# Two blocks on one core: the second block's two attentions as sequences of small tasks, and a margin on modelled times in the order of the first half's parts

## The chip, the cores and the metric

The kernel runs on one core of a Trainium2 chip. The metric is the time of one execution on the device in microseconds (us), lower is better. Each time below is from the chip: either a timed run, or one execution taken with the hardware profiler. The engines are named as in the profile: PE is TensorE's matrix multiply, PEld its weight load, DVE is VectorE, ACT ScalarE, POOL GpSimd, SP the engine whose queue issues nearly all DMAs.

## What is computed

1024 tokens of width 1024 go through two transformer blocks in float32. Block 1 mixes a recurrent branch with an attention branch and ends in a mixture of 32 experts; the change does not touch it. Block 2, cut to what matters:

```python
xn = rmsnorm(x, attn_norm_g)
qa, ka, va, qb, kb, vb, f_logit = split(xn @ w_in)          # 8 heads of 64 each; ka, va: 2 heads
out_a = swa_sinks_attention(rms(qa), rms(ka), va, sinks)    # window of 128 keys, a sink logit per head
out_b = forgetting_attention(rms(qb), rms(kb), vb, log_f)   # causal, logit += c[t] - c[s], c = cumsum(log_f)
x = x + concat(out_a, out_b) @ w_out
x = x + square(relu(rmsnorm(x) @ w_up)) @ w_down            # d_ff 4096
```

## The kernel before

**Matmuls.** Each float32 operand of a matmul is split into a rounded high half and a rounded remainder, and a product is three matmuls: high x high, high x low, low x high (`mm3`), accumulated in a bank of PSUM. The split is one copy on ScalarE and then one subtraction on VectorE (`split`, `split_T`), so each operand that TensorE reads has passed ScalarE and VectorE first, in that order. Weights stream from HBM by way of SP's queue in pieces of 512 KB and are split in the same way (128x1024 rows of the trace).

**The order.** The program's order on each engine is made when it is built. The kernel is written as tasks (Python generators with a priority, lower goes first). A task yields either a time or a condition. `Tasks.run` takes again and again the first task, by priority, whose condition holds and whose time is not after "now", the planner's clock of TensorE. That clock comes from a cost model with a fixed price for each instruction; `model.written(ap)` is the modelled time at which an operand is ready, `model.released(ap)` the time at which it may be overwritten. So `yield W(t.f())` before a matmul means: put it into the order only when TensorE's clock has come to the operand's modelled time. Until then parts of other tasks are put there; the main task (dense matmuls, priority 9) nearly always has one. `Later` holds back instructions of the other engines, and DMAs, in the same way until the model says that they are ready. On the chip each engine works through its own queue in that order, and waits where an operand is later than was modelled.

**Block 2.** The tokens go in two halves of 512. The main task (`block2`) runs the projections of half 0 (`kvf`, `kb`, `qb`, `vb`, `qa`), then those of half 1, and stores the results in DRAM (`d_kva`, `d_kb`, `d_qb`, `d_qa` and others). Beside it run tasks:

- `fox(0)`, priority 1, the forgetting attention of half 0. It starts when `qb` and `vb` are done. Per pair of heads (4 pairs) and pair of query blocks (2) it makes scores (matmuls of 64 rows), adds a bias row that is loaded from `d_cb` and masked by GpSimd, takes the exponential, and hands two pieces (one for each head) to `fox_values`. That task, priority 1, scales a piece by the reciprocal of its sum (VectorE), waits, transposes its probabilities in chunks of 256 keys (TensorE, into banks 4 and 5), splits them, multiplies them with V, and stores the output to `d_mix`. 16 pieces in a half. Four probability buffers (`p`) go round between the two tasks.
- `swa(0)`, priority 2, the windowed attention of half 0. It starts when `qa` is done, and is one task: for each of the four blocks of 128 queries the scores of both groups of heads, then `values` of group 0, `values` of group 1, then the next block's scores. `values` scales, waits, transposes one or two chunks, waits, multiplies, waits, and stores the output to `d_mix`: 8 stores in a half. Two probability buffers (`nsr = 2`).
- `forget(1)`, priority 1: the cumulated log of the forget gates of half 1, written to `d_cb`.
- `mixin(0)`, priority 4, added when `vb` of half 1 is done. It allocates 8192 words in one piece (`TT`), loads the eight tiles of `d_mix` one after the other and splits them. With it done, `out2(0)` may run in the main task: the output projection, which stands after the first two of the four `qa` tiles of half 1. Its matmuls stand in TensorE's queue in order, and nothing else of the main task can go ahead of it.

Then the last two `qa` tiles follow, and the MLP of half 0 (`mlp`), with `swa(1)`, after it `fox(1)`, and `mixin(1)` beside it. `fox(1)` needs the flag `swa1`. Then come `out2(1)` and the MLP of half 1, with no attention beside it.

On-chip memory is handed out by arenas: `F` (19872 words a partition, plain float32), `R` (16896 words, rounded) and two swing arenas `Z` (8192 words each) that `R` falls back on. A task starts only when `fits` says that its buffers can be had. While both attentions of half 0 run, `swa(0)` holds 6144 words of one swing arena, and the other one holds half 1's input.

The windowed attention's main loop before:

```python
        yield from prep(n0)
        for n in range(n0, n0 + 5):
            if n > n0 and nsr == 2:
                for kh in range(2):
                    yield from values(n - 1, kh)
            if n < n0 + 4:
                yield from scores(n)
                if n + 1 < n0 + 4:
                    yield from prep(n + 1)
```

Of the kernel before, what the change touches and what calls it, by code (L numbers as in the profile page):

```python
# [657 lines left out]
class Kern:  # L658
# [1348 lines left out]
    def block2(self):  # L2007
# [60 lines left out]
        for half in range(2):  # L2068
# [95 lines left out]

    def swa(self, half):
# [10 lines left out]
        S, tb, ob = Banks(self.psum, 2, 2), Banks(self.psum, 4, 2), self.bank(6)  # L2176
# [5 lines left out]
        st, orr = Ring(F, 4, 32), Ring(F, 1, 512)  # L2182
        self.sp.dma_start(kv.f(nk, 256), self.KVA[k0 * 128:(n0 + 4) * 128].rearrange("(a p) c -> p a c", p=128))
        qs, Q, P = {}, {}, {}
# [21 lines left out]
        sr = Ring(F, nsr, 1024)  # L2206
# [12 lines left out]
        def scores(n):  # L2219
# [5 lines left out]
            bs, ss = [sr.next(), sr.next()], [st.next(), st.next()]  # L2225
# [19 lines left out]
            for kh in range(2):  # L2245
                P[n, kh] = (bs[kh], ss[kh], w)

        def values(n, kh):
            b, s, w = P.pop((n, kh))
# [19 lines left out]
            for c in range(nb):  # L2269
                vv = V.r(nk, 2, 128)[:, n + 1 - nb + c - k0, kh]  # L2270
                self.mm(ob, vv, ts[c].r(2, 512)[:, 0], c == 0, False)
                self.mm(ob, vv, ts[c].r(2, 512)[:, 1], False, c == nb - 1)
            yield W(ob)
            t = orr.next()
# [5 lines left out]
        yield from prep(n0)  # L2280
        for n in range(n0, n0 + 5):
            if n > n0 and nsr == 2:
                for kh in range(2):
                    yield from values(n - 1, kh)
            if n < n0 + 4:
                yield from scores(n)
                if n + 1 < n0 + 4:
                    yield from prep(n + 1)
            if n > n0 and nsr == 4:
                for kh in range(2):  # L2290
                    yield from values(n - 1, kh)
        for b in (kT, V, qr, qT, sr, pt, st, orr) + ((bias, snk, g) if half else ()):
# [3 lines left out]
    def fox(self, half):  # L2296

        F, R, v, act, gp = self.F, self.R, self.v, self.act, self.gp
        W, free = self.model.written, self.model.released
# [14 lines left out]
        steps = [(pr, gi, hh) for pr, gi in units for hh in range(2)]  # L2314
        self.tasks.add(self.fox_values(half, steps, fx), 1)
# [59 lines left out]
        for n, (pr, gi) in enumerate(units):  # L2375
# [32 lines left out]
            for hh in range(2):  # L2408
                fx["ready"][2 * n + hh] = (ss[hh], out[hh])
# [5 lines left out]
    def fox_values(self, half, steps, fx):  # L2415
        F, R, v, act, gp = self.F, self.R, self.v, self.act, self.gp
        W, free = self.model.written, self.model.released
        NKB = 4 * (half + 1)
# [410 lines left out]
```

## Time and profile before

| | us |
|---|---|
| median of 3 timed runs (lowest, highest) | 2784.4 (2781.36, 2788.27) |
| the profiled execution, its own time | 2780.47 |
| span of that execution, first to last instruction | 2778.7 |
| mean granted clock of TensorE over the span | 0.979 |

The profile is of one execution. A busy time of an engine is the sum of its instructions' durations; PE's are pipelined, so that a PE that is always busy shows 100%. The granted clock is the share of TensorE's full clock that the chip let through in a stretch: 1.00 is 2.4 GHz, 0.50 is 1.2 GHz, and a value between them is a stretch that had both. Times in the timelines count from the start of the span. L234 and L270 are lines of the helper that records every instruction, so nearly all rows carry one of these two lines and are told apart by operands and shapes. Operands are named by their arena: `rounded` is R, `swing` Z, `exact` F, `psum` PSUM; names that begin with `d_` are tensors in DRAM.

In the trace, matmuls `psum<-rounded,swing 128x512` are the projections and `out2`, `psum<-rounded 64x..` are scores of the forgetting attention, `psum<-rounded 128x128` and `128x256` its multiplications with V, `psum<-swing 64x..` scores of the first half's windowed attention, `psum<-swing 128x512` its multiplications with V, and `psum<-exact 128x128` transposes.

### The profile page before, as it was taken

How to read it: one execution, taken by the hardware profiler on the slowest of the kernel's cores; microseconds unless marked ns; L12 is line 12 of the kernel's file. 1: busy time of each engine (PE TensorE's matmuls, PEld its weight loads, DVE VectorE, ACT ScalarE, POOL GpSimd, SP SyncE). 2: the span in 40 equal slices, each digit the busy share in tenths (PEclk: the TensorE clock that was granted, in tenths of full speed). 3: DMA queues.
4: the chain of work that ended last, by engine and by line, in shares of the span. 5: the costliest groups of instructions: out<-in, count | busy, mean ns of one | idle time of the engine just before them, and what ended most of it. 6: DMA issues, size and time to landing. Idle time of an engine off the chain costs nothing. (4 is left out here: it accounts for less than half of the span.)

```text
span 2778.7 us, 37066 instructions
## 1 busy us (share of the span) xinstructions
PE 2642.0 (95%) x13090; PEld 2146.4 (77%) x13090; DVE 1785.0 (64%) x3100; ACT 1507.8 (54%) x2455; POOL 422.5 (15%) x486
## 2 busy tenths in 40 slices
PE   8899999999999799999997898889999999999999
PEld 6677777778888678888886776667887778888887
DVE  4574443652575699999986647755666666546683
ACT  4144444543443588888886646645545555345542
POOL 0540002430121113111111322200000000000000
PEclk9999999999999899999999999899999999999999
DMA  5333223435556899999997444444234443443330
GB/s 180 119 98 92 92 74 106 133 107 174 192 178 226 281 344 376 373 361 358 365 358 261 165 143 138 128 146 150 88 113 145 132 144 120 148 140 122 122 120 32
DMA packets 272030, 496.22 MB, mean 179 GB/s; under 512 B 30337, under 2 KB 127265, under 8 KB 271841
## 3 DMA queue, kind: packets, MB, share of 16 engines
q1 hardware_dynamic: 261184, 471.78, 49.7%
q0 software_dynamic: 9216, 16.81, 2.4%
q10 hardware_dynamic: 1440, 5.24, 0.5%
q8 instruction: 103, 1.69, 0.3%
q14 instruction: 87, 0.70, 0.1%
HBM read 440.05 MB, written 70.45 MB: 184 GB/s over the span
## 5 line engine op out<-in xcount | busy, mean ns | idle before, releaser
L234 PE MATMUL psum<-rounded,swing 128*128 128x512 f32 (+1 forms) x3552 | 868.4, 396 | 23.4 <-ACT swing L270 10.3
L234 PE MATMUL psum<-rounded 128*128 128x512 f32 (+6 forms) x3672 | 791.8, 386 | 24.3 <-DVE rounded L270 11.3
L234 PE MATMUL psum<-swing,rounded 128*128 128x512 f32 (+1 forms) x3328 | 785.0, 389 | 0.4 <-DVE swing L270 0.4
L234 PEld LDWEIGHTS psum<-rounded,swing 128*128 128x128 f32 x3552 | 651.5, 192 | 166.3 <-issue 18.4
L234 PEld LDWEIGHTS psum<-rounded 128*128 128x128 f32 (+1 forms) x3672 | 609.4, 189 | 174.0 <-issue 19.8
L270 DVE TENSOR_TENSOR rounded<-exact,rounded 128x1024 fp32r<-128x1024 f32 (+1 forms) x483 | 572.2, 1206 | 234.4 <-ACT rounded L270 226.8
L234 PEld LDWEIGHTS psum<-swing,rounded 128*128 128x128 f32 x3328 | 603.8, 189 | 129.2 <-issue 6.5
L270 ACT ACTIVATE rounded<-exact 128x1024 fp32r<-128x1024 f32 (+1 forms) x483 | 500.6, 1045 | 296.6 <-PE psum L234 221.1
L234 PE MATMUL psum<-exact 128*128 128x128 f32 (+6 forms) x2198 | 312.9, 284 | 78.0 <-DVE exact L270 23.4
L234 PEld LDWEIGHTS psum<-exact 128*128 128x128 f32 (+2 forms) x2198 | 262.5, 163 | 141.4 <-DVE exact L270 36.1
L270 POOL TENSOR_TENSOR exact<-exact 128x1 f32<-128x1 f32 (+6 forms) x272 | 261.2, 964 | 721.4 <-DMA exact<-d_cb 416.6
L270 ACT ACTIVATE exact<-psum 128x512 f32<-128x512 f32 (+4 forms) x290 | 160.1, 553 | 366.0 <-PE psum L234 297.3
L270 ACT ACTIVATE exact<-exact 128x512 f32<-128x512 f32 (+11 forms) x398 | 247.1, 632 | 175.7 <-DVE exact L270 147.4
L270 DVE TENSOR_TENSOR rounded<-swing,rounded 128x1024 fp32r<-128x1024 f32 x217 | 256.4, 1218 | 37.9 <-ACT rounded L270 37.0
L270 ACT ACTIVATE rounded<-swing 128x1024 fp32r<-128x1024 f32 x217 | 223.8, 1065 | 36.3 <-PE psum L234 26.4
L270 DVE TENSOR_TENSOR exact<-psum,exact 128x512 f32<-128x512 f32 x156 | 107.3, 688 | 143.3 <-PE psum L234 111.8
L270 DVE TENSOR_TENSOR exact<-exact 128x512 f32<-128x512 f32 (+9 forms) x250 | 154.6, 628 | 42.4 <-POOL exact L270 24.1
L270 DVE CUSTOM_DVE_ANT_0 exact<-psum,exact 128x512 f32<-128x512 f32 (+5 forms) x224 | 127.8, 593 | 80.4 <-PE psum L234 51.6
L270 POOL TENSOR_SCALAR exact<-exact 128x1 f32<-128x1 f32 (+4 forms) x134 | 42.6, 318 | 785.4 <-DVE exact L270 553.1
L270 DVE TENSOR_TENSOR swing<-psum,swing 128x512 fp32r<-128x512 f32 (+2 forms) x151 | 88.9, 615 | 95.1 <-ACT swing L270 94.7
L270 ACT ACTIVATE rounded<-psum 128x512 fp32r<-128x512 f32 (+2 forms) x190 | 88.1, 496 | 105.8 <-PE psum L234 105.2
L270 DVE TENSOR_TENSOR rounded<-psum,rounded 128x512 fp32r<-128x512 f32 (+2 forms) x190 | 101.7, 558 | 56.4 <-ACT rounded L270 56.3
(49 smaller groups left out, 1074.1 us busy)
## 6 DMA issues: line engine op xcount, KB each, us to landing
exact<-in_w_dram SPq DMA_DIRECT2D x188, 512.0 KB
swing<-in_w_dram SPq DMA_DIRECT2D x186, 512.0 KB
exact<-in_w_in_dram SPq DMA_DIRECT2D x72, 512.0 KB
exact<-in_w_down_dram SPq DMA_DIRECT2D x66, 512.0 KB
exact<-in_w_up_dram SPq DMA_DIRECT2D x62, 512.0 KB
exact<-in_w_out_dram SPq DMA_DIRECT2D x32, 512.0 KB
exact<-in_x_dram SPq DMA_DIRECT2D x16, 512.0 KB
d_g<-exact SPq DMA_DIRECT2D x32, 256.0 KB
```

The lines of the kernel that those rows point to most:

```text
L234: r = fn(*args, **kw)
L270: r = fn(*args, **kw)
```

## The change

It makes five edits, all of them in the order of the work:

1. `safe(half)`: in half 0, `W` is the operand's modelled time plus 600 ns, in the scores of both attentions and in both `values` tasks. In half 1 it stays as it was.
2. `swa` becomes three tasks: scores (priority 2), `swa_scale` (1) and `swa_values` (1), with four probability buffers instead of two.
3. `fox_values` gives its scaling to a task of its own, `fox_scale` (1). Neither scaling task has the margin.
4. In both `values` tasks a chunk's multiplication comes after the next chunk's transposes, and an output's evacuation (`finish`) after the transposes that follow its last multiplication; where the next piece is not scaled yet, both are done at once.
5. `mixin(0)` is added right after `qa` of half 0, and waits for `swa0` alone.

The diff, cut to its core:

```diff
--- before.py
+++ after.py
@@ -2085,7 +2085,6 @@
             if half == 0:
                 self.tasks.add(self.fox(0), 1)
             else:
-                self.tasks.add(self.mixin(0), 4)
                 nq = 2
...
             self.flag(f"qa{half}")
             if half == 0:
                 self.tasks.add(self.swa(0), 2)
+                self.tasks.add(self.mixin(0), 4)
...
+    def safe(self, half):
+
+        return self.model.written if half else lambda ap: self.model.written(ap) + 600.0
+
     def swa(self, half):
...
-        W, free = self.model.written, self.model.released
+        W, free = self.safe(half), self.model.released
...
-        nsr = 2
+        nsr = 4
...
-        yield lambda: (self.has(f"qa{half}") and self.ws.settled() and self.F.fits(256 * nk, 512, 512, 32, 32, 32, 32, 512, *[1024] * nsr) and
+        yield lambda: (self.has(f"qa{half}") and self.ws.settled() and self.F.fits(256 * nk, 512, 512, 32, 32, 32, 32, 512, *[1024] * (nsr - nk // 4)) and
...
-        sr = Ring(F, nsr, 1024)
+        sr = Slots(F, nsr, 1024)
+        sx = {"V": V, "k0": k0, "nk": nk, "sr": sr, "st": st, "pt": pt, "orr": orr, "ready": {}, "scaled": {}}
+        steps = [(n, kh) for n in range(n0, n0 + 4) for kh in range(2)]
+        self.tasks.add(self.swa_scale(steps, sx), 1)
+        self.tasks.add(self.swa_values(half, steps, sx), 1)
...
             for kh in range(2):
-                P[n, kh] = (bs[kh], ss[kh], w)
-
-        def values(n, kh):
-            b, s, w = P.pop((n, kh))
+                sx["ready"][n, kh] = bs[kh], ss[kh], w
+
+        yield from prep(n0)
+        for n in range(n0, n0 + 4):
+            yield from scores(n)
+            if n + 1 < n0 + 4:
+                yield from prep(n + 1)
...
+    def swa_scale(self, steps, sx):
+
+        v, act, snk, W = self.v, self.act, self.snk, self.model.written
+        for n, kh in steps:
+            yield lambda: (n, kh) in sx["ready"]
+            b, s, w = sx["ready"].pop((n, kh))
             f = s.f()
             x = b.f(4, 256)[:, :, :w]
             yield W(f)
...
             v.tensor_tensor(x, x, f[:, 12:16, None].to_broadcast([128, 4, w]), OP.mult)
-            yield W(b.f())
-            nb = w // 128
-            ts = []
-            for c in range(nb):
-                p, t = tb.next(), pt.next()
-                yield free(p)
-                for j in range(4):
-                    self.pe.transpose(p[:, j * 128:j * 128 + 128], b.f(4, 256)[:, j, c * 128:c * 128 + 128], self.ident)
-                self.split_T(p, t.r(2, 512)[:, 0], t.r(2, 512)[:, 1], t.f(2, 512)[:, 0])
-                ts.append(t)
-            yield max(W(ts[-1].f()), free(ob))
...
+            sx["st"].give(s)
+            sx["scaled"][n, kh] = b
+
+    def swa_values(self, half, steps, sx):
...
+        for n, kh in steps:
+            nb = 2 if n else 1
+            for c in range(nb):
+                if (n, kh) not in sx["scaled"]:
+                    yield from finish()
+                    yield from multiply()
+                    yield lambda: (n, kh) in sx["scaled"]
+                b = sx["scaled"][n, kh]
+                p, t = tb.next(), pt.next()
+                yield max(free(p), W(b.f()))
+                for j in range(4):
+                    self.pe.transpose(p[:, j * 128:j * 128 + 128], b.f(4, 256)[:, j, c * 128:c * 128 + 128], self.ident)
+                self.split_T(p, t.r(2, 512)[:, 0], t.r(2, 512)[:, 1], t.f(2, 512)[:, 0])
+                if c == nb - 1:
+                    sx["sr"].give(b)
+                yield from finish()
+                yield from multiply()
+                state[0] = (n, kh), c, nb, t
+        yield from finish()
+        yield from multiply()
+        yield from finish()
...
     def fox(self, half):
...
-        W, free = self.model.written, self.model.released
+        W, free = self.safe(half), self.model.released
...
+        fx["scaled"] = {}
+        self.tasks.add(self.fox_scale(steps, fx), 1)
         self.tasks.add(self.fox_values(half, steps, fx), 1)
...
+    def fox_scale(self, steps, fx):
+
+        v, W = self.v, self.model.written
         for n, (pr, gi, hh) in enumerate(steps):
             yield lambda: n in fx["ready"]
...
             v.reciprocal(f[:, 4:6], f[:, 2:4])
             for ii in range(2):
                 x = bs[ii].f()[:, :(i0 + ii + 1) * 128]
                 v.tensor_scalar(x, x, f[:, 4 + ii:5 + ii], None, op0=OP.mult)
-            yield W(bs[1].f())
             fx["st"].give(s)
+            fx["scaled"][n] = bs
+
+    def fox_values(self, half, steps, fx):
...
+        def multiply():
+            if state[0] is None:
+                return
+            (pr, gi, hh), c0, t0 = state[0]
+            state[0] = None
...
+            yield max(W(t0.f()), free(o) if c0 == 0 else 0.0)
+            for j, z in ((0, 0), (1, 0), (1, 1), (0, 1)):
+                q0 = 128 if end and j == 1 else 0
+                self.mm(o[:, q0:256], V[:, c0 + j, hh], t0.r(2, 512)[:, z, 256 * j + q0:256 * j + 256], c0 + j == 0 and z == 0,
+                        end and j == 0 and z == 1)
...
+        for n, c in chunks + [(None, None), (None, None)]:
+            if n is not None:
...
+                if n not in fx["scaled"]:
+                    yield from finish()
+                    yield from multiply()
+                    yield lambda: n in fx["scaled"]
...
+                yield max(free(p), W(bs[0].f()), W(bs[1].f()))
...
+            yield from finish()
+            yield from multiply()
+            if n is not None:
+                state[0] = steps[n], c, t
...
     def mixin(self, half):
...
-        yield lambda: self.has(f"swa{half}") or self.has(f"fox{half}0")
+        yield lambda: self.has(f"swa{half}") or half and self.has(f"fox{half}0")
```

`finish` holds the evacuation that stood at the end of `values` before: one copy on ScalarE, one addition on VectorE, one store to `d_mix`. `swa_values` has a `multiply` of the same form as that of `fox_values`.

## Rows read from the trace of the kernel before

**Rows 1.** The page, part 1: busy us (share of the span) xinstructions, TensorE.

```profile
PE 2642.0 (95%) x13090; PEld 2146.4 (77%) x13090; DVE 1785.0 (64%) x3100; ACT 1507.8 (54%) x2455; POOL 422.5 (15%) x486
```

**Rows 2.** Busy time by stage of block 2; length first, then engines, granted clock, DMA.

```profile
1624.70:1663.00 38.30, 33.64 (x159) 26.30 (x157) 18.15 (x48) 17.95 (x42) 9.90 (x14) 0.91 0.58 168
1663.00:1803.00 140.00, 116.13 (x669) 92.25 (x668) 108.44 (x320) 90.17 (x236) 37.85 (x50) 0.92 0.47 132
1803.00:1847.00 44.00, 43.39 (x223) 35.08 (x221) 25.28 (x60) 22.68 (x48) 1.83 (x2) 0.99 0.40 129
1847.00:1870.00 23.00, 15.34 (x50) 10.84 (x51) 9.95 (x14) 6.38 (x11) 2.20 (x2) 0.70 0.64 214
...
1920.00:1950.00 30.00, 26.80 (x127) 21.31 (x126) 13.24 (x33) 16.83 (x35) 0.25 (x1) 0.89 0.50 163
1950.00:2361.00 411.00, 404.13 (x2135) 325.63 (x2133) 272.68 (x569) 212.57 (x405) 15.92 (x32) 1.00 0.40 123
```

**Rows 3.** Waits of PE from 1624 to 1816 us: total, times, longest.

```profile
PE psum L234 <- DVE rounded L270: 17.0, 12, 3.3
PE psum L234 <- DVE exact L270: 3.9, 3, 1.6
PE psum L234 <- DVE swing L270: 3.7, 5, 1.8
PE psum L234 <- ACT rounded L270: 3.6, 1, 3.6
```

**Rows 4.** Busy time in three windows of ten us, columns as above.

```profile
1740.00:1750.00 10.00, 6.88 (x24) 5.22 (x22) 8.18 (x22) 6.33 (x13) 3.12 (x6) 0.66 0.76 223
...
1850.00:1860.00 10.00, 4.40 (x10) 2.94 (x11) 3.61 (x6) 1.89 (x3) 2.20 (x2) 0.50 0.66 227
1870.00:1880.00 10.00, 10.00 (x46) 8.29 (x45) 3.84 (x4) 3.19 (x3) 0.00 (x0) 1.00 0.13 32
```

**Rows 5.** Timeline of PE: start, length, instructions [idle before, releaser].

```profile
1667.89 0.51 PE L234 MATMUL psum<-rounded 128*128 128x256 f32 x2 [0.47 <-DVE rounded L270]
...
1674.61 0.89 PE L234 MATMUL psum<-swing 64*128 64x128 f32 x12
...
1743.76 0.80 PE L234 MATMUL psum<-rounded 128*128 128x128 f32 x2 [3.12 <-DVE rounded L270]
...
1798.70 0.91 PE L234 MATMUL psum<-rounded 128*128 128x128 f32 x2 [3.29 <-DVE rounded L270]
...
1814.34 1.24 PE L234 MATMUL psum<-rounded 128*128 128x256 f32 x8
...
1836.56 1.08 PE L234 MATMUL psum<-swing 128*128 128x512 f32 x4
...
1857.46 2.93 PE L234 MATMUL psum<-rounded,swing 128*128 128x512 f32 x6 [5.60 <-ACT swing L270]
```

**Rows 6.** Timeline of DVE before the matmuls of 1743.76.

```profile
1741.47 0.56 DVE L270 CUSTOM_DVE_ANT_0 exact<-psum,exact 128x384 f32<-128x384 f32 x1 [0.67 <-POOL exact L270]
...
1741.95 1.22 DVE L270 TENSOR_TENSOR rounded<-exact,rounded 128x1024 fp32r<-128x1024 f32 x1
1743.09 0.61 DVE L270 TENSOR_TENSOR rounded<-psum,rounded 128x256 fp32r<-128x256 f32 x2
```

**Rows 7.** Waits of POOL for bias rows, 1624 to 1816 us.

```profile
POOL exact L270 <- DMA exact<-d_cb: 59.7, 29, 9.6
```

**Rows 8.** Timeline of SP's queue: stores to and loads from `d_mix`.

```profile
1657.32 0.48 SPq L221 DMA_DIRECT2D d_mix<-exact  x1
...
1818.01 0.46 SPq L221 DMA_DIRECT2D d_mix<-exact  x1
...
1838.64 0.42 SPq L221 DMA_DIRECT2D exact<-d_mix  x1
...
1853.93 5.20 SPq L221 DMA_DIRECT2D exact<-d_mix  x3
```

**Rows 9.** Timeline of ACT: the first split of `mixin(0)`.

```profile
1844.56 0.63 ACT L270 ACTIVATE swing<-exact 128x512 fp32r<-128x512 f32 x1 [2.38 <-DMA exact<-d_mix]
```

More of the change, by code (lines that the diff above doesn't have):

```diff
@@ L2224, in scores @@
             ks = slice(e - w, e)
-            bs, ss = [sr.next(), sr.next()], [st.next(), st.next()]
+            bs, ss = [], []
+            for kh in range(2):
+                bs.append((yield from sr.take()))
+                ss.append((yield from st.take()))
             for z in range(2):
@@ L2245, in scores @@
             for kh in range(2):
-                P[n, kh] = (bs[kh], ss[kh], w)
-        def values(n, kh):
-            b, s, w = P.pop((n, kh))
+                sx["ready"][n, kh] = bs[kh], ss[kh], w
[4 more added lines that the diff above has]
+                yield from prep(n + 1)
+        for b in (kT, qr, qT) + ((bias, g) if half else ()):
+            b.free()
+    def swa_scale(self, steps, sx):
[3 more added lines that the diff above has]
+            b, s, w = sx["ready"].pop((n, kh))
             f = s.f()
@@ L2278, in values @@
                               t.f(4, 128)[0:64])
[L2280 to L2292, printed above, removed]
+        for n, kh in steps:
[11 more added lines that the diff above has]
+                self.split_T(p, t.r(2, 512)[:, 0], t.r(2, 512)[:, 1], t.f(2, 512)[:, 0])
+                if c == nb - 1:
+                    sx["sr"].give(b)
[5 more added lines that the diff above has]
+        yield from finish()
+        for b in (V, sx["sr"], pt, sx["st"], sx["orr"]) + ((self.snk,) if half else ()):
             b.free()
@@ L2408, in fox @@
             for hh in range(2):
-                fx["ready"][2 * n + hh] = (ss[hh], out[hh])
+                fx["ready"][2 * n + hh] = (ss[hh], out[hh], 4 * half + 2 * gi)
             if n + 1 < len(units):
@@ L2413, in fox @@
             b.free()
[L2415 to L2418, printed above, removed]
-        tb, o = Banks(self.psum, 4, 2), self.bank(7)[:, 0:256]
-        pt, orr = Ring(R, 2, 1024), Ring(F, 1, 256)
+    def fox_scale(self, steps, fx):
+        v, W = self.v, self.model.written
         for n, (pr, gi, hh) in enumerate(steps):
             yield lambda: n in fx["ready"]
-            s, bs = fx["ready"].pop(n)
+            s, bs, i0 = fx["ready"].pop(n)
             f = s.f()
-            i0 = 4 * half + 2 * gi
-            nb = i0 + 2
             yield W(f)
@@ L2463, in fox_values, with multiply, finish @@
-            done = gi == 1 and hh == 1
-            if done:
-                fx["V"].give(fx["vv"].pop(pr))
+            fx["scaled"][n] = bs
+    def fox_values(self, half, steps, fx):
+        F, R, v, act = self.F, self.R, self.v, self.act
+        W, free = self.safe(half), self.model.released
+        NKB = 4 * (half + 1)
+        tb, o = Banks(self.psum, 4, 2), self.bank(7)[:, 0:256]
+        pt, orr = Ring(R, 2, 1024), Ring(F, 1, 256)
+        chunks = [(n, c) for n, (pr, gi, hh) in enumerate(steps) for c in range(0, 4 * half + 2 * gi + 2, 2)]
+        state = [None, None]
+        def multiply():
+            if state[0] is None:
+                return
+            (pr, gi, hh), c0, t0 = state[0]
+            state[0] = None
+            end = c0 == 4 * half + 2 * gi
+            V = fx["vv"][pr].r(NKB, 2, 128)
+            yield max(W(t0.f()), free(o) if c0 == 0 else 0.0)
[3 more added lines that the diff above has]
+                        end and j == 0 and z == 1)
+            if end:
+                state[1] = pr, gi, hh
+                if gi == 1 and hh == 1:
+                    fx["V"].give(fx["vv"].pop(pr))
+        def finish():
+            if state[1] is None:
+                return
+            pr, gi, hh = state[1]
+            state[1] = None
@@ L2466, in fox_values @@
             yield W(o)
-            t = orr.next()
+            t, q = orr.next(), (4 * half + 2 * gi) * 128
             act.activation(t.f()[0:64], o[64:128], AF.Copy)
```

77 lines of the change are left out of this document (39 added, 38 removed).

## The prediction

> **What bounds the kernel now.** I read the page first. TensorE is busy 95% of the span [rows 1], so what can be won is its idle time and the time it runs at half clock. The table by stage [rows 2] shows where these lie inside block 2. A stage's idle time is its length minus PE busy; what the clock costs is PE busy times (1 - granted clock), since work at the lower of the two levels (1.2 instead of 2.4 GHz) takes twice as long. Idle plus clock, in us: 1624.7 to 1663 (the first half's forgetting attention) 4.7 + 3.0; 1663 to 1803 (both attentions under the second half's projections) 23.9 + 9.3; 1803 to 1847 0.6 + 0.4; 1847 to 1870 (start of `out2(0)`) 7.7 + 4.6; 1920 to 1950 (start of the second half's windowed attention) 3.2 + 2.9; 1950 to 2361 (the rest of the second half's attentions, under the MLP) 6.9 + 0. The change touches nothing else. So at most 67 us are in reach, 46 of them between 1663 and 1870, and only 13 in the second half.
>
> The waits of TensorE up to 1816 us [rows 3] say who made the idle time: 28.2 us in 21 waits, 24.6 of them for VectorE, the longest 3.6 us. The ten-microsecond windows [rows 4] show the granted clock at 0.66 at 1740 and at 0.50 at 1850, around the longest waits, and at 1.00 at 1870, under unbroken dense matmuls. TensorE's timeline [rows 5] shows two kinds of place. First, pairs of 128x128 matmuls behind waits of 3.12 and 3.29 us: the multiplications with V that end a piece of `fox_values`, waiting for the low half of the transposed probabilities (five such waits, 9.8 us). Second, the start of `out2(0)`, whose matmuls of 1857.46 come 5.60 us after the work ahead of them.
>
> The first kind is a VectorE queue that ran later than the planner thought. TensorE had been given the multiplication of 1743.76 at 1740.6. VectorE meanwhile [rows 6] waited for GpSimd, which itself spends 59.7 us in 29 waits on bias rows from `d_cb` [rows 7]; a 1.22 us weight split came next; the halves that TensorE waited for ran at 1743.09, last.
>
> The second kind is the end of `swa(0)`. Its first scores stand at 1674.61 and its last multiplication at 1836.56, while `fox(0)` had its last at 1814.34 [rows 5]. `mixin(0)` needs 8192 words in one piece, which only the end of `swa(0)` sets free, so its first load is issued at 1838.64 and the eight follow one by one, the last three from 1853.93 [rows 8]. From the first load to its split on ScalarE are 5.9 us (1838.64 to 1844.56) [rows 8, 9].
>
> **The change part by part.** No arithmetic is added or taken away: the same matmuls, transposes, exponentials and stores, in another order. So each part is costed by the waits it moves.
>
> *The margin of 600 ns in half 0.* A part whose operand is due at t goes into TensorE's queue when the planner's clock passes t + 0.6 us; dense matmuls (46 in 10 us [rows 4]) stand in its place. A wait of length w loses min(w, 0.6). The 21 waits lose at most 12.6 us; their mean is 1.3 us, so most lose all of the 0.6. Lower bound 0, if VectorE only falls further behind. I take 11.
>
> *Multiply and finish held back.* In both `values` tasks the multiplication of a chunk now comes after the next chunk's transposes, and the evacuation of an output after the next transposes too. For the five waits above that is about one step of 0.6 us more and some tenths of a microsecond of transposes. Upper bound 9.8 - 5 x 0.6 = 6.8, lower 0; I take 4.
>
> *Clock.* Between 1624.7 and 1803 it costs 12.3 us. If the waits shrink to half, about 5 come back (0 to 12).
>
> *`swa` in three tasks, four probability buffers instead of two, `mixin(0)` added right after `qa0`.* Before, a block of 128 queries went through scores, values of head group 0, values of group 1, and only then the next scores: 162 us for four blocks, 40 us each [rows 5]. Each group waited in turn for its scaling, transposes, multiplication and output. Now scores and scaling run ahead, multiplication and output behind, and only the transposes stand in the chain. I take 30 us a block, which ends `swa(0)` near 1795; any value under 35 ends it before `fox(0)`. Then `mixin(0)` loads its four tiles while `fox(0)` goes on, and each head pair's as it ends; after the last pair one load of 5.9 us is left. This can give back the 12.3 us of 1847 to 1870. But after 20 us less of waits and clock ahead of it `out2(0)` wants to start near 1826 instead of 1847, and `fox(0)`'s last store is issued at 1818.01 [rows 8]: with the load behind it 1824, plus the landing of the store. That fits only just, so I take 10; lower bound 0.
>
> *Work displaced.* With four buffers `forget(1)` (2144 words) finds no room until `swa(0)` is done. Only `fox(1)` needs it, which waits for all of `swa(1)`, so it costs nothing and leaves VectorE freer near 1760. The start of `swa(0)` asks for 5760 words where, by the sizes in the code, some 6500 are free; if they were not, it would wait for `fox(0)`'s end. The loads of `mixin(0)` and the stores are the same DMAs, earlier on SP's queue and issued when the planner holds them ready, so what stands behind them (weight loads of dense work) is not held up longer than before.
>
> *Second half.* No margin there. The pipelined order can take some of the 13 us; more parts in flight can add as much. I take 2 (bounds -5 to +10).
>
> *New waits.* With the chains side by side, operands of more tasks stand in one VectorE queue that is busy 108 of 140 us [rows 2]; squeezed into 115 us it would be busy 94%. No row shows that order; the window at 1740 had VectorE at 0.82 and TensorE idle for 3.1 us of ten [rows 4]. Bounds 0 and the 11 us of the margin; I charge 4, nearer to nothing, since the work is spread by the margin.
>
> The Trainium skill speaks against the change here: "PSUM — Partial Sum Buffer", Engine vs sequencer instructions, says that ScalarE, VectorE and GpSimd take their queues strictly first in, first out. At 1740 the trace agrees: the awaited halves ran behind a bias wait and a weight split. By this rule a delay on TensorE's side frees no place in VectorE's queue, and a late bias now holds up both attentions; the sum would keep the tail and some clock alone and come to 2770, rival B below.
>
> The sum: 11 + 4 + 5 + 10 + 2 - 4 = 28 us. The profiled execution took 2780.5 us (span 2778.7), so 2752.5; the median of the three runs lies 3.9 us above it, and I give 2755 for the median.
>
> The Trainium skill would judge the headroom otherwise: "Perfetto Trace Analysis", Identifying the Most-Contended Engine, says to go by LDWEIGHTS busy share, not by matmul busy time. Pure dense work shows 8.29 of 10 [rows 4]; the 207 us from 1663 to 1870 hold 138.2 [rows 2], as much as 167 us at that share. An estimate by that page: 40 us in reach there instead of 46, which leaves the sum as it is.
>
> **The rivals.** *A, the attention tail (slower).* The margin is paid in `fox(0)`'s chain, at up to four steps a piece (scores, transposes, multiplication, output), 16 pieces: 16 x 4 x 0.6 = 38 us. `fox(0)` would end at 1854 instead of 1816, the dense work would be used up near 1825, and TensorE would wait for the last pair's 8 us of store and load: `out2(0)` in full flow at 1862 instead of 1857.5, after a wait that leaves it at half clock for some 5 us more: +9, about 2794. It decides from a `fox(0)` that ends 34 us later. For it: the chain is all latency, and `out2(0)` stands ahead of the other dense tiles in the main task, so nothing fills. Against it: a group's transposes no longer wait for the multiplication and output of the one before, which frees probability slots sooner.
>
> *B, VectorE only shifts.* Margin and reordering give nothing net, the tail gives its 10 and the clock 4: 2784.4 - 14 = 2770. For it: VectorE's waits on GpSimd and `d_cb` stay [rows 7]. Against: TensorE's waits are short, 1.3 us in the mean.
>
> *C, nothing to measure.* What the projections gain is waited for again ahead of `out2(0)`: `fox(0)` ends 20 to 30 us later than it did, `out2(0)` is in full flow within 8 us of 1857.5: 2776 to 2792, about 2782.
>
> **How the numbers follow.** Chances: forecast 0.58 (its own range 2742 to 2767), B 0.18, C 0.12, A 0.12. About 0.3% (8.4 us) is what a measurement of this kernel can tell from no change, so faster means under 2776. Faster: 0.58 and all but a little of B, 0.75; same: C and that little, 0.13; slower 0.12. The range for 8 in 10 goes down to 2733, where the bounds of margin, reordering, clock and tail and most of the second half are had (12.6 + 6.8 + 12 + 12.3 + 8 = 52), and up to 2785, which takes in B and most of C and leaves A out.
>
> **What would show it.** Right: no multiplication of `fox(0)` behind a wait of 3 us; TensorE's waits between 1624 and `out2(0)` at 10 to 15 us together; `swa(0)`'s last store before `fox(0)`'s; loads from `d_mix` beginning near 1800; `out2(0)` in full flow near 1830 without a gap of 5 us; a clock above 0.95 throughout. Wrong: a gap of over 10 us ahead of `out2(0)`; `fox(0)`'s 16 stores spread over more than the 161 us from 1657.32 to 1818.01 [rows 8]; new waits in the second half.

## The result and the profile after

The changed kernel is slower: 2819.6 us (median of 4 runs, 2817.9 to 2821.4) against 2785.7 for the kernel before on the same chip, a ratio of 1.0123 (95% interval 1.0106 to 1.0141). The forecast was 2755 with a range up to 2785, so sign and range are both wrong. The profiled execution has a span of 2819.6 us; counted from the first load from `d_cb` (the start of `fox(0)`) to the end it takes 1184.6 us, 32 more than before (1152.4).

First the page's busy line of after (TensorE), then its table by stage: length, then PE, PEld, DVE, ACT, POOL busy, granted clock, DMA share, GB/s. The limits are moved to where the same work stands.

```profile
PE 2669.7 (95%) x13090; PEld 2171.0 (77%) x13090; DVE 1782.9 (63%) x3100; ACT 1511.5 (54%) x2455; POOL 428.4 (15%) x486
```

```profile
1633.00:1672.00 39.00, 35.57 (x172) 27.98 (x171) 18.39 (x48) 19.57 (x43) 10.23 (x15) 0.91 0.55 158
1672.00:1846.00 174.00, 144.59 (x758) 115.87 (x759) 128.78 (x378) 105.10 (x276) 35.60 (x49) 0.82 0.42 124
1846.00:1857.00 11.00, 11.00 (x51) 9.10 (x50) 0.69 (x1) 1.96 (x4) 0.00 (x0) 1.00 0.30 105
1857.00:1935.00 78.00, 78.00 (x362) 64.91 (x361) 43.39 (x47) 34.56 (x45) 11.23 (x16) 1.00 0.53 171
1935.00:2045.00 110.00, 92.24 (x469) 72.27 (x467) 72.97 (x200) 60.25 (x147) 1.70 (x2) 0.92 0.33 101
2045.00:2310.00 265.00, 255.24 (x1384) 203.01 (x1383) 177.51 (x363) 140.27 (x252) 18.05 (x30) 0.99 0.42 134
```

The same share of busy time as in [rows 1], 95%, hides the loss: PE is "busy" 28 us longer with the same 13,090 instructions, at a mean granted clock of 0.970 instead of 0.979. By stage, against [rows 2]: the hole ahead of `out2(0)` (0.70 clock, 15.34 of 23 us busy) is gone, 1846 to 1935 is dense at 1.00. But 1672 to 1846 has 29 us of idle time at a clock of 0.82, where the same work had 24.5 at 0.92 to 0.99; and the second half's windowed attention (1935 to 2045), which had 6 us of idle time and clock, now has 18 us idle at 0.92.

TensorE's waits of after, first 1632 to 1863, then 1942 to 2045 us: total, times, longest.

```profile
PE psum L234 <- DVE exact L270: 15.5, 10, 3.3
PE psum L234 <- DVE swing L270: 7.9, 7, 2.7
PE psum L234 <- DVE rounded L270: 6.9, 4, 3.8
PE psum L234 <- ACT rounded L270: 1.7, 1, 1.7
PE psum L234 <- ACT exact L270: 0.4, 1, 0.4
...
PE psum L234 <- DVE exact L270: 8.4, 5, 3.4
PE psum L234 <- DVE swing L270: 6.2, 3, 2.9
```

In the first half 32.4 us stand against 28.2 [rows 3], with another make-up: 17.0 for `DVE rounded` has become 6.9, 3.9 for `DVE exact` has become 15.5. But [rows 3] end at 1816, ahead of the tail. Up to 1863 one line of before is new and one longer, and its sum is 36.4:

```profile
PE psum L234 <- ACT swing L270: 6.8, 2, 5.6
PE psum L234 <- DVE swing L270: 5.1, 6, 1.8
```

So waits have moved from the tail into the attentions; their sum over the half has not grown in this profile. What a wait is for is inferred from its pair of operands. A transpose reads `exact`, so where it waits for a DVE instruction that writes `rounded` or `swing`, it waits for the split of an earlier chunk: for a PSUM bank to be read out. A multiplication reads `rounded` or `swing`; where it waits for `exact`, it waits for the evacuation of the last output. Scores that wait for `exact` wait for a score bank. Sorted like that: multiplications waiting for their own operand 9.8 us (5 waits) before, 0 after; waits for a PSUM bank 13.6 us before (transposing banks 10.6, score banks 3.0), 26.2 after (transposing 14.5, output 8.8, scores 2.9). Transposes that wait for `DVE exact`, their own scaled probabilities, stand at 0.9 us before and 4.2 after. Some of the waits for banks, and the end of the attentions, in TensorE's timeline of after:

```profile
1681.33 1.12 PE L234 MATMUL psum<-exact 128*128 128x128 f32 x4 [3.82 <-DVE rounded L270]
...
1756.95 1.19 PE L234 MATMUL psum<-swing 128*128 128x512 f32 x2 [3.32 <-DVE exact L270]
...
1840.13 1.10 PE L234 MATMUL psum<-rounded 128*128 128x256 f32 x8
1841.07 66.15 PE L234 MATMUL psum<-rounded,swing 128*128 128x512 f32 x291
...
1970.74 1.38 PE L234 MATMUL psum<-rounded 64*128 64x256 f32 x12 [0.56 <-DVE exact L270]
1974.97 1.12 PE L234 MATMUL psum<-exact 128*128 128x128 f32 x4 [2.86 <-DVE swing L270]
...
2017.63 0.73 PE L234 MATMUL psum<-swing,rounded 128*128 128x512 f32 x2 [3.35 <-DVE exact L270]
```

66 us of dense matmuls run without a gap behind the last multiplication of `fox(0)`, `out2(0)` among them; in [rows 5] 5.60 us of idle time stood there. And SP's queue of after shows the loads that begin before the attentions end:

```profile
1792.91 0.42 SPq L221 DMA_DIRECT2D exact<-d_mix  x1
...
1844.62 0.45 SPq L221 DMA_DIRECT2D d_mix<-exact  x1
1847.68 0.35 SPq L221 DMA_DIRECT2D exact<-d_mix  x1
```

Why a bank comes free late is seen at 1974.97. The four transposes want a bank whose last contents were written by transposes at 1969.15. ScalarE's and VectorE's timelines of after:

```profile
1970.32 0.51 ACT L270 ACTIVATE exact<-exact 128x256 f32<-128x256 f32 x1 [0.59 <-DVE exact L270]
...
1970.83 0.57 ACT L270 ACTIVATE exact<-psum 128x512 f32<-128x512 f32 x1
1971.43 0.63 ACT L270 ACTIVATE exact<-exact 128x512 f32<-128x512 f32 x1
1972.10 0.63 ACT L270 ACTIVATE swing<-exact 128x512 fp32r<-128x512 f32 x1
1972.63 0.49 ACT L270 ACTIVATE exact<-exact 128x256 f32<-128x256 f32 x1
...
1973.13 0.49 ACT L270 ACTIVATE exact<-exact 128x256 f32<-128x256 f32 x1
...
1973.62 1.05 ACT L270 ACTIVATE swing<-psum 128x512 fp32r<-128x512 f32 x2
```

```profile
1974.22 1.29 DVE L270 TENSOR_TENSOR swing<-psum,swing 128x512 fp32r<-128x512 f32 x2 [0.77 <-ACT swing L270]
```

The copies that begin to empty the banks run at 1973.62, behind three exponentials of scores that ran ahead (128x256) and three steps of a dense evacuation (128x512), and VectorE waits for them. The Trainium skill's "PSUM — Partial Sum Buffer", Engine vs sequencer instructions, says that these engines take their queues strictly first in, first out; the trace agrees for ScalarE, which works without a gap from 1970.32 to the copies at 1973.62, and TensorE's wait of 2.86 us is the price here.

### The profile page after: what moved, and what is told of

Read it like the earlier page. It is cut to its first block, busy times and chain, and to the rows that moved or that the text cites. A ratio compares the mean times of both kernels' runs of the same rounds, so it can differ in the third digit from the quotient of the medians.

```text
span 2819.6 us, 37106 instructions
## 1 busy us (share of the span) xinstructions
PE 2669.7 (95%) x13090; PEld 2171.0 (77%) x13090; DVE 1782.9 (63%) x3100; ACT 1511.5 (54%) x2455; POOL 428.4 (15%) x486
## 5 line engine op out<-in xcount | busy, mean ns | idle before, releaser
L234 PE MATMUL psum<-rounded 128*128 128x512 f32 (+6 forms) x3672 | 796.9, 388 | 20.4 <-DVE exact L270 14.8
L234 PE MATMUL psum<-swing,rounded 128*128 128x512 f32 (+2 forms) x3328 | 796.8, 392 | 9.6 <-DVE exact L270 7.8
L270 DVE TENSOR_TENSOR rounded<-exact,rounded 128x1024 fp32r<-128x1024 f32 (+2 forms) x483 | 571.7, 1206 | 240.1 <-ACT rounded L270 230.4
L270 ACT ACTIVATE rounded<-exact 128x1024 fp32r<-128x1024 f32 (+2 forms) x483 | 501.1, 1046 | 331.2 <-PE psum L234 264.1
L234 PE MATMUL psum<-exact 128*128 128x128 f32 (+6 forms) x2198 | 329.1, 291 | 92.6 <-DVE exact L270 35.3
L234 PEld LDWEIGHTS psum<-exact 128*128 128x128 f32 (+2 forms) x2198 | 271.7, 167 | 160.0 <-DVE exact L270 37.1
L270 ACT ACTIVATE rounded<-swing 128x1024 fp32r<-128x1024 f32 x217 | 224.0, 1065 | 35.8 <-PE psum L234 25.8
L270 DVE TENSOR_TENSOR rounded<-psum,rounded 128x512 fp32r<-128x512 f32 (+2 forms) x190 | 102.6, 558 | 54.9 <-ACT rounded L270 54.3
```

The source lines that it names most:

```text
L234: r = fn(*args, **kw)
L270: r = fn(*args, **kw)
```

## The experiments

Fifteen kernels beside after. Each ratio is against runs of the kernel before on the same chip. For each profile the loss is summed as in the prediction, idle time plus PE busy x (1 - clock), in windows of 5 us. "First half" is from 10 us before the first load from `d_cb` to 15 us before the second from `d_kva`, tail ahead of `out2(0)` included; "swa(1)" from there to the second half's first load from `d_kb`; "fox(1)" to 5 us after the last store to `d_mix`. The columns are in us. On the chip of e1 to e4 the kernel before took 2779.2 us, on the others 2784.4 to 2785.7, so kernels are compared by their ratios.

| kernel | ratio (95%) | first half | swa(1) | fox(1) |
|---|---|---|---|---|
| before | 1 | 51.6 | 6.0 | 6.8 |
| after | 1.0123 (1.0106, 1.0141) | 60.8 | 24.8 | 11.2 |
| e1 margin alone | 1.0047 (1.0030, 1.0064) | 57.6 | 2.5 | 9.2 |
| e2 after, no margin | 1.0185 (1.0153, 1.0217) | 66.0 | 30.4 | 12.0 |
| e3 after, margin in both halves | 1.0107 (1.0082, 1.0132) | 61.1 | 18.4 | 8.2 |
| e4 after, windowed attention as before | 1.0033 (1.0016, 1.0049) | 50.3 | 2.6 | 16.0 |
| e5 e3 and a margin on releases | 1.0065 (1.0049, 1.0082) | 52.9 | 17.4 | 15.2 |
| e6 after, two buffers | 1.0062 (1.0043, 1.0081) | 56.5 | 7.8 | 12.5 |
| e7 after, two output banks | 1.0118 (1.0100, 1.0136) | 61.4 | 25.5 | 11.0 |
| e9 after, 2.5 us margin in swa | 1.0076 (1.0059, 1.0092) | 60.7 | 11.3 | 14.0 |
| e10 after, swa(1) as before | 1.0065 (1.0048, 1.0083) | 59.9 | 5.3 | 12.1 |
| e11 before, `out2(0)` a tile later | 0.9993 (0.9980, 1.0005) | 46.1 | 6.3 | 8.5 |
| e12 e4 without margin | 1.0125 (1.0103, 1.0147) | 77.0 | 6.9 | 12.0 |
| e13 before, held back alone | 1.0077 (1.0056, 1.0099) | 69.1 | 4.1 | 13.8 |
| e14 before, scaling task alone | 1.0060 (1.0038, 1.0082) | 57.7 | 4.1 | 11.4 |
| e15 before, swa(0) at priority 0 | 1.0041 (1.0026, 1.0055) | 59.0 | 4.1 | 12.0 |
| e16 before, swa split alone | 1.0094 (1.0070, 1.0118) | 54.9 | 25.8 | 7.6 |

The three columns account for the time: their sum, less that of before, agrees within 3 us in each profile with the time from the first load from `d_cb` to the end, less that of before (after: 32.4 against 32.2). So no more than that was lost outside these stages.

Each row is one profiled execution, and kernels with the same order show how far a column can be trusted. after, e3, e7 and e10 have the same order in the first half: 59.9 to 61.4. before, e1, e11 and e15 have the same code in the second half: 2.5 to 6.3 in swa(1), 6.8 to 12.0 in fox(1). Differences of that size in a column are not read as effects.

Two theories stood at the start. **P**: the margin covers operands, and the waits have moved to the banks, which it doesn't cover. **S**: the chains side by side press the attentions into a shorter stretch, where ScalarE and VectorE can't keep up and too few dense matmuls stand between. The first expectations also name Q, that the margin itself is what costs, and R, that the second half lacks it.

**Margin: e1, e2, e3, e5.**

e1 adds `safe` to the kernel before; e2 and e3 change its one line in the kernel after; e5 adds to e3 the same 600 ns on releases:

```diff
-        return self.model.written if half else lambda ap: self.model.written(ap) + 600.0
+        return self.model.written                              # e2
+        return lambda ap: self.model.written(ap) + 600.0       # e3, e5
...
-        W, free = self.safe(half), self.model.released
+        W, free = self.safe(half), lambda ap: self.model.released(ap) + 600.0   # e5
```

> The kernel before with the margin of 600 ns on the operands' times in the first half, in scores, transposes and multiplications of both attentions; both attentions as they were. Theory P (the margin does what it says, and the loss comes from the finer tasks, whose waits are for PSUM banks that the margin does not cover): the 17 us that TensorE waits for rounded halves up to 1816 us shrink to 8 to 12, nothing else changes: 2775 to 2783 against 2785.7. Rival Q (the margin itself delays the attentions and so costs): 2790 or more.

> The changed kernel with the margin taken out, so that only the new tasks and their order are left. Theory P: the second half stays as in the changed kernel, and in the first half waits for operands come back beside the waits for banks: 2820 to 2835. Rival Q (the margin is what costs): 2795 to 2810.

> The changed kernel with the margin of 600 ns in the second half too. Rival R (the second half lost its 24 us because its finer tasks have no margin): 2793 to 2803. Theory P (its waits are for banks, to which the margin does not apply): 2810 to 2822.

> The run with the margin in both halves, and the 600 ns on the release of PSUM banks too, in both halves. Theory P (TensorE waits for banks because the margin does not cover their release): the 31 us of waits for banks in the first half and the 8.6 us in the second half's windowed attention fall by a third or more; ratio to the kernel before 1.000 to 1.006, against 1.011 without it. Theory S (the chains side by side set more attention into a stretch than ScalarE and VectorE can follow, whatever TensorE waits for): the waits only change their name; 1.008 to 1.014.

Measured: 2793.7 (e1), 2830.7 (e2), 2810.1 (e3), 2802.2 (e5). Alone the margin costs 0.5%: the waits for operands of multiplications fall from 9.8 to 2.3 us, but TensorE's waits up to the end of the attentions (1862) are 35.4 us instead of 28.2, and the attentions end later, so that most of the hole ahead of `out2(0)` stays (7.4 us of idle time and clock, 11.1 before). So Q holds for the margin alone. Nor are all waits for operands shorter: transposes that wait for their scaled probabilities cost 8.4 us in e1, 0.9 before. Two of them in TensorE's timeline of e1:

```profile
1763.46 1.09 PE L234 MATMUL psum<-exact 128*128 128x128 f32 x8 [1.87 <-DVE exact L270]
...
1858.32 1.97 PE L234 MATMUL psum<-exact 128*128 128x128 f32 x8 [2.60 <-DVE exact L270]
```

In the new order the margin gains, against Q: 1.0185 without, 1.0123 with. R falls with e3, which stays above its range (2803 us, a ratio of 1.0062). A margin on releases gains some 0.4% more from e3 to e5, with intervals that just touch; in the profiles the first half gains 8 us (61.1 to 52.9) and `fox(1)` loses 7. That goes P's way, but it leaves half of the loss, and the ratio lies between the ranges of P and S.

**The windowed attention: e4, e6, e7, e9, e10, e16.**

```diff
# e4: swa of the kernel before, with the margin; e10: the same in the second half alone, without it
-        nsr = 4
+        nsr = 2                                                # e6
...
-        tb, ob = Banks(self.psum, 4, 2), self.bank(6)
+        tb, obs = Banks(self.psum, 4, 2), Banks(self.psum, 6, 1 + half)         # e7
...
-        W, free = self.safe(half), self.model.released
+        W, free = lambda ap: self.model.written(ap) + 2500.0, self.model.released   # e9, swa alone
```

e16 is after with `fox` and its helpers of the kernel before, and no margin; `mixin(0)` is early in it too.

> The changed kernel with the windowed attention as it was, one serial task with two probability buffers, but with the margin in the first half; the forgetting attention in its new order. Theory P in the form that the finer windowed attention is the cause (it makes the dense bursts of small matmuls from 1700 to 1760 and from 1960 to 2020): 2778 to 2792. If the forgetting attention's new order is the cause: 2808 or more.

> The changed kernel with two probability buffers in the windowed attention instead of four, so that the next block's scores begin only when the last block's probabilities have been transposed: nearly serial again, though still in three tasks. Theory S: the windowed attention takes 150 us or more again in either half, the waits in the second half fall from 17.5 to under 8 us, and the ratio to 1.003 to 1.007 (that of the serial task). Theory P: multiplications and transposes still share their banks at short distance: 1.009 to 1.013.

> The changed kernel with two output banks instead of one in the second half's windowed attention (the bank of the forgetting attention is idle then). Theory P: the 4.2 us of waits of its multiplications for the output bank go, and with them some low clock; 3 to 6 us faster than the changed kernel, ratio 1.010 to 1.011. Theory S: they turn into other waits; no change, 1.0115 to 1.013.

> The changed kernel with a margin of 2.5 us instead of 0.6 and 0 on the operands of the windowed attention, in both halves, which spreads it over more dense work. Theory S: waits and low clock go down in both halves, the second half's windowed attention to under 8 us of waits and clock together (24.8 in the changed kernel); ratio 0.998 to 1.004. Theory P: the waits for banks stay, 1.008 or more. If the first half's windowed attention now ends after the dense work, a wait ahead of the output projection shows it.

> Theory S (the windowed attention, compressed into half its stretch, is what costs in the second half): with the serial windowed attention back in the second half alone, idle plus clock between 1930 and 2075 us falls from 24.8 to about 6 us, so the ratio to the kernel before falls from 1.0123 to 1.005 to 1.007 (2800 to 2805 us). Rival P (the compression in the first half has used up work that the second half lacks, or the forgetting attention of the second half takes the waits over): the waits go elsewhere, ratio 1.009 or more.

> The kernel before with the windowed attention in three tasks and four buffers and the operand loads of the output projection early, the forgetting attention as before, no margin. If the edits add up (1.0185 for both new orders, 1.0125 for the forgetting attention's): ratio 1.004 to 1.008, the loss in the second half's windowed attention (some 15 to 20 us there against 6 before) partly paid by the missing tail. If it is the two together that crowd VectorE: ratio 1.002 or less.

Measured: 2790.4 (e4), 2799.7 (e6), 2818.5 (e7), 2805.7 (e9), 2802.0 (e10), 2809.4 (e16). The column swa(1) settles the second half: it is 25 to 30 us wherever four buffers go round with no margin there, with either forgetting attention (e16: 25.8), 17 to 18 with 600 ns (e3, e5), 11 with 2.5 us (e9), and 2.5 to 8 with two buffers or the serial form. e6 keeps the three tasks and takes away only the running ahead; e10 takes back the whole edit there. Either is worth about half of the loss (1.0062 and 1.0065 against 1.0123). e4, with the serial form in both halves, takes back 0.9%: the first half gains 10 us as well (50.3). The windowed attention of the second half in three kernels, columns as above: after, e6, e10.

```profile
1942.00:2030.00 88.00, 70.25 (x367) 54.73 (x366) 62.51 (x187) 51.39 (x136) 0.00 (x0) 0.90 0.22 66
```

```profile
1935.00:2041.00 106.00, 99.44 (x521) 78.37 (x520) 75.97 (x202) 62.89 (x152) 0.00 (x0) 0.98 0.31 94
```

```profile
1942.00:2086.00 144.00, 139.96 (x709) 114.04 (x708) 93.42 (x221) 80.06 (x175) 0.00 (x0) 0.99 0.31 92
```

About the same attention work is done in 88, 106 and 144 us; VectorE is busy 71, 72 and 65% of it, so its mean load is not what separates after from e6. What differs is how much dense work stands in between (367, 521 and 709 matmul instructions in all), and in after 18 us of idle time come with it. e7 gives the output a second bank, the object of the longest wait there (3.35 us, at 2017.63); the stage stays at 25.5, with the waits now for transposing banks (7.2), score banks (6.2) and the operands of scores (3.6). So the waits only changed their object, as S expected; the ratio alone (1.0100 to 1.0136) can't tell its range from P's. One bank is not the bound. That the chain of ScalarE and VectorE behind all the banks is, the rows at 1973.62 show for one wait; for the others it is inferred.

S missed some of its marks: e6 needs 106 us there and not 150, and e9 reached 11.3 us and 1.0076 where S had under 8 and at most 1.004. e16 lies above both of its ranges (25.8 us where 15 to 20 were expected).

**The forgetting attention: e12, e13, e14.**

e12 is e4 without the margin. (e4, e12 and e13 also add `mixin(0)` earlier, to no effect: its loads can't begin before the serial `swa(0)` gives up its memory, and in e12 and e13 they begin at 1863 and 1866.) e13 puts the scaling back into `fox_values`. e14 makes it a task and leaves the rest of `fox_values` as it was; its edit in `fox_values`:

```diff
-            s, bs = fx["ready"].pop(n)
-            f = s.f()
+            bs = fx["scaled"][n]
...
-            yield W(f)
-            v.reciprocal(f[:, 4:6], f[:, 2:4])
...
             yield W(bs[1].f())
-            fx["st"].give(s)
```

> The kernel before with the new order of the forgetting attention alone (scaling task, multiplication and evacuation held back), no margin, serial windowed attention. If the margin costs by itself, as when added to the kernel before (1.0047): ratio 0.998 to 1.001, below the 1.0033 of the same kernel with the margin. If the margin helps in the new order, as it did with the windowed attention split in three (1.0185 without, 1.0123 with): ratio 1.005 to 1.009.

> The kernel before with the forgetting attention's multiplication and evacuation held back, its scaling in the values task as before, no margin. Theory H (the parts held back keep output and transposing banks longer and cost): ratio 1.008 or more, near the 1.0125 of both edits. Rival K (the scaling task costs, since its multiplications go into VectorE's queue ahead of the splits that release banks): ratio 1.004 or less.

> The kernel before with the forgetting attention's scaling in a task of its own, multiplication and evacuation where they stood. Theory K: ratio 1.008 or more, waits of TensorE for releases of transposing banks above 15 us in the first half (10.6 before). Rival H: ratio 1.004 or less, those waits near 10.6 us.

Measured: 2817.3 (e12), 2806.6 (e13), 2800.6 (e14). The surprise is e12: this order alone, without margin, costs as much as the whole change, above both ranges of its expectation, and nearly all of it in the first half (77.0 against 51.6). Both its edits cost, 0.8 and 0.6%, together about as much as e12; neither H nor K alone is right (e13 is just under H's 1.008, e14 between 1.004 and 1.008). TensorE's waits of e12 from 1625 to 1864 us:

```profile
PE psum L234 <- DVE rounded L270: 14.5, 10, 4.2
PE psum L234 <- DVE exact L270: 14.0, 11, 3.1
PE psum L234 <- DVE swing L270: 7.4, 3, 3.6
```

Sorted as above, transposing banks take 20.6 us, score banks 10.2, operands of multiplications 2.2. e13 has 18.5 for transposing banks and 6.9 for outputs, which it keeps longer; e14 has 12.4 and 5.9 for score banks, so that K's mark for it (above 15 for transposing banks) was missed, and its time falls between the two.

**The start of `out2(0)`: e11, e15.**

```diff
-                nq = 2
+                nq = 3                                         # e11
...
-                self.tasks.add(self.swa(0), 2)
+                self.tasks.add(self.swa(0), 0)                 # e15
```

> The kernel before, with three instead of two projection tiles ahead of the output projection of the first half. Theory T (the tail of 11 us ahead of the output projection is a lack of dense work, and the changed kernel paid for removing it with more waits than it was worth): the tail goes and nothing else moves, 8 to 12 us less, ratio 0.995 to 0.997. Rival U (the third tile only delays what comes behind, or the wait returns at the weights): ratio 0.999 or more.

> The kernel before with the first half's windowed attention at priority 0 instead of 2. If the tail ahead of the output projection can be had by ending the windowed attention first: it ends before the forgetting attention, the loads of the output projection's operands begin before 1820 us, and the ratio is 0.995 to 0.998. If the forgetting attention only ends as much later, or VectorE's queue turns the gain into waits: 0.999 or more.

Measured: 2782.1 (e11), 2795.5 (e15). In e11 the hole shrinks and moves instead of closing; in TensorE's timeline of e11:

```profile
1857.24 3.01 PE L234 MATMUL psum<-rounded,swing 128*128 128x512 f32 x12 [1.41 <-ACT exact L270]
1862.51 1.22 PE L234 MATMUL psum<-rounded,swing 128*128 128x512 f32 x3 [2.26 <-ACT swing L270]
1865.18 34.47 PE L234 MATMUL psum<-rounded,swing 128*128 128x512 f32 x138 [1.45 <-ACT swing L270]
```

The eight loads still begin at 1844 and end at 1864, since `swa(0)` still holds the memory, so a tile of cover is not enough: the ratio is U's, not T's. It is the only kernel here not slower than before. In e15 the higher priority doesn't end `swa(0)` first: its scores still run at 1820, the loads begin at 1854.

## Why the prediction was wrong

In the profiles a gain of 28 us was forecast and a loss of 32 measured: 35 us of the difference lie in the first half (26 gained on paper, 9 lost), 25 in the second.

**The margin (11 us).** This is the first step that failed: "a wait of length w loses min(w, 0.6)". It took the 21 waits for a fixed list, each of which shrinks. Of the 28.2 us, 9.8 were waits of multiplications for their operand and 4.5 of scores and transposes for theirs, which the margin covers; 13.6 were for banks, which it doesn't. A new order makes a new list: in after the 9.8 are gone, as forecast, and 12.6 us more for banks have come, and the mark of 10 to 15 us in all was missed with 32.4 (38.0, 38.2 and 38.9 in e3, e7 and e10, with the same order there). In e1, with no other edit, the list grew to 35.4.

**Multiply and finish held back (4 us).** Sign wrong. What was costed was the operand they wait for; what they keep occupied meanwhile was not. Alone it costs 0.8% (e13).

**The clock (5 us).** Sign wrong, and not by way of the sum of the waits, as the step had it: over the first half idle time is 32.8 us instead of 36.8, and the clock costs 28.0 instead of 14.8. In e3, e7 and e10 idle time is 38.1 to 39.1 and the clock costs 20.8 to 22.9. So in this half, against the one profile of before, idle time is about what it was, and the loss is the clock's. It lies in the stage from 1672 to 1846, at 0.82; why so much of that stage ran at the lower level is open.

**The tail (10 us).** Right in place and size: 7.7 + 3.4 us before, 0 after, with the loads from 1792.91 and no gap at 1841. But `fox(0)`'s last multiplication came at 1840.13 instead of 1814.34, 26 us later, 9 of which the profiles already stand apart at the start of `fox(0)`. What the tail gave was paid ahead of it, in waits and above all in the clock: the whole first half lost 9 us net.

**The second half (2 us gained, bounds -5 to +10).** The largest miss: 12.8 us of idle time and clock became 36.0. Of the 23 us, 19 are the windowed attention. The step read the second half as safe because it had little to lose (13 us); but that it had little idle time was no bound on what an edit can add. e6, e10 and e16 show what added it: four buffers running ahead. The margin missing there is a smaller part (600 ns get back 6 of 25 us in e3, 2.5 us get back 14 in e9). The rows of after, e6 and e10 fit a loss of cover, the attention done in 88 us instead of 144 with about half as many matmuls in all; that this is how it costs is argued from them.

**New waits (4 us, bounds 0 and 11).** The right mechanism, with a bound that doesn't hold. It was tied to the 11 us that the margin was to give; nothing ties it to that, since new waits can exceed the ones removed. The step also charged VectorE's share alone; the row at 1973.62 shows ScalarE's queue ahead of it.

**The rivals.** A had the side, not the cause: `out2(0)` doesn't wait. B's premise, that a later TensorE frees no place in VectorE's queue, is nearest to what happened, but it reckoned with no net loss. Of the marks of "right", the ones of the tail came (loads from 1792.91, no gap ahead of `out2(0)`), and so did the one that no multiplication of `fox(0)` waits 3 us. Of the marks of "wrong", two came: stores of `fox(0)` over 172 us (1672.25 to 1844.62) and new waits in the second half.

P and S are both in part right: most of TensorE's waits are for banks, and running ahead is what brings them in the second half (e6, e10, e16). Open is why e13 and e14 each cost in the first half, where e4, with both and the margin, has 50.3 us, less than before (its loss shows in `fox(1)`, 16.0 in this one profile, where others with the same code have 11.0 to 14.0). That the margin takes back most of what this order costs (1.0125 to 1.0033), while in the old order it costs 0.5% itself, is shown; the reason is not.

## What to carry to other kernels

Before costing a wait away, say what it is a wait for (operand, or a buffer to be read out) and what else the change keeps occupied meanwhile; a margin or a later place can help only the kind it names. A chain that runs ahead doesn't raise the rate of the engines behind it: here it brought the same evacuations in a shorter stretch with less dense work between. A stage with little idle time can gain little from an edit and still lose much, so the bound on the loss has to come from the change, not from the idle time that the stage has now.

## What the runs showed of the hardware

The busy share of a stretch is itself a product of the clock. Two windows of 20 us, of after and of e12:

```profile
1700.00:1720.00 20.00, 15.96 (x80) 12.01 (x77) 15.81 (x63) 13.03 (x45) 1.91 (x5) 0.61 0.40 101
```

```profile
1760.00:1780.00 20.00, 14.52 (x85) 11.22 (x83) 14.99 (x37) 10.85 (x25) 5.09 (x6) 1.00 0.34 85
```

The first looks busier (15.96 against 14.52 us), but it ran mostly at 1.2 GHz, the second at 2.4 throughout. At a granted clock of 0.61 its 15.96 us are the work of 9.7 us at the full clock (15.96 x 0.61, an estimate), so it held less work and not more.

Idle time and the price of the clock are not to be read apart from each other either. Four profiles with the same order in the first half (after, e3, e7, e10) have 32.8, 38.1, 38.4 and 39.1 us of idle time there, and the clock costs 28.0, 22.9, 22.9 and 20.8: the one with the least idle time pays the most, and the sum stays between 59.9 and 61.4. The one profile of before had 36.8 and 14.8 in the same half.
